# Masked softmax on one core: GpSimd zeroes a slot before, not after, it issues the two whole loads

## The chip, the cores and the metric

The kernel runs on one core of one Trainium2 chip. The metric is the time of one execution on the device in microseconds; lower is better. For a profiled execution the page also gives the span, from the first to the last recorded event.

## The reference

Input `x` has the shape (16, 8, 256, 256), float32; `lengths` holds 16 whole numbers, drawn from 128 to 255. For each batch only the first `lengths[b]` columns take part, the others of the result are zero:

```python
result = np.zeros_like(x)
for b in range(batch):
    length = lengths[b]
    masked = x[b, :, :, :length].copy()
    masked = masked - np.max(masked, axis=-1, keepdims=True)
    exp_masked = np.exp(masked)
    result[b, :, :, :length] = exp_masked / np.sum(exp_masked, axis=-1, keepdims=True)
```

The draw is fixed. The lengths are 188 233 229 243 195 252 165 210 222 180 209 157 159 199 214 248.

## The kernel before, in words

A batch is one tile: 2048 rows, 16 on each of 128 partitions, 256 columns; 2.10 MB. The tile `xt` has 8 slots for such tiles. Batches are worked on by position: positions 0, 1, 2 are batches 1, 2, 3, position 3 is batch 0, and from position 4 on position and batch agree (`batch_of`). Everything is done in place in the slot.

**Loads.** SyncE issues position 0 in two halves (L136), which go through its DMA queue, q1 of the profile. GpSimd issues positions 1 and 2 as whole tiles (L175); its queue is q0. From position 3 on GpSimd loads only as many columns as the batch needs, in steps of 8 or 16 (`pick`, L154): it reads the length, branches to one of several written-out DMAs, and issues it. For such a narrow load the columns from 160 on are first zeroed in the slot (`fill`, L179), once for each of the slots 3 to 7. The zero fill of slot 3 comes after GpSimd has waited for `s_v` to reach 2 (VectorE's two steps L219 and L227, which set up `down` and `len_s`). Position 3 needs slot 3's fill, positions 4 and on need all five fills. In the loop over later positions (L189) a load waits until the load two positions before has landed (`s_sw`), and until the store of the tile that had the slot before has landed (`s_st`).

**Work.** VectorE sets columns past the length to a very low value (`mask`, L236), ScalarE takes the exponential row by row with the row's sum (`rows`, L343, 16 instructions for a tile, in two halves), VectorE takes the reciprocal of the sums (L257) and multiplies (L260, once for each half). VectorE's order is written out: it multiplies position b's first half, masks position b+1, multiplies b's second half; for position 1 the mask comes first. A final check of the sums (L292 to L303) decides on a second, slower path, which is not taken here.

**Stores.** SyncE issues them (L143) in position order, through q1 as well: position 0 in halves, positions 1 to 7 as a half and two quarters, 8 to 12 and 15 in halves, 13 and 14 whole. A store waits for its multiply (`s_out`) and, from position 2 on, for the landing of the store two positions before (L142).

The lines the change touches, in the order of GpSimd's program:

```python
for b in range(1, ahead):
    nc.gpsimd.dma_start(out=xt[:, b], in_=x_f[batch_of(b)]).then_inc(s_ld[b + 1], 16)
nc.gpsimd.wait_ge(s_v, 2)
def fill(b):
    nc.gpsimd.memset(xt[:, b, :, low:], 0.0).then_inc(s_fill, 1)
fill(ahead)
```

with `ahead = 3` and `low = 160`.

Of the kernel before, what the change touches and what calls it, by code (L numbers as in the profile page):

```python
# [21 lines left out]
def kernel(  # L22
# [6 lines left out]
    nc = tc.nc  # L29
# [9 lines left out]
    x_f = x.rearrange("b h q k -> b (h q) k").rearrange("b (p t) k -> b p t k", p=P)  # L39
# [5 lines left out]
    ahead = 3  # L45
    assert ahead == 3 and slots == 8 and batch == 16

    def batch_of(pos):
        return pos + 1 if pos < ahead else 0 if pos == ahead else pos
# [22 lines left out]
    xt = pool.tile([P, slots, nt, seq_k], F32, name="xt")  # L72
# [26 lines left out]
    with tc.tile_critical(no_gpsimd_drain=True):  # L99
# [4 lines left out]
        s_ld = [sem(f"s_ld{k}") for k in range(ahead + 1)]  # L104
# [32 lines left out]
        for b in range(batch):  # L137
            s_b = s_st[b % 2]
            for s in parts(b):
                nc.sync.wait_ge(s_out, 2 * b + (s.stop - 1) // half + 1)  # L140
                if b >= 2 and s.start == 0:
                    nc.sync.wait_ge(s_b, 64 * (b // 2 + 1))  # L142
                nc.sync.dma_start(  # L143
                    out=out_f[batch_of(b), :, s, :], in_=xt[:, b % slots, s, :]
# [26 lines left out]
        nc.gpsimd.memset(ones_c, 1.0).then_inc(s_ones, 1)  # L171
        for par in range(2):
            nc.gpsimd.memset(seed[:, par : par + 1], 0.0).then_inc(s_st[par], 64)  # L173
        for b in range(1, ahead):
            nc.gpsimd.dma_start(out=xt[:, b], in_=x_f[batch_of(b)]).then_inc(s_ld[b + 1], 16)  # L175
        nc.gpsimd.wait_ge(s_v, 2)

        def fill(b):
            nc.gpsimd.memset(xt[:, b, :, low:], 0.0).then_inc(s_fill, 1)  # L179

        fill(ahead)
        nc.gpsimd.wait_ge(s_word, 16)
        nc.gpsimd.wait_ge(s_fill, 1)
        v_len = length(POOL, word[0:1, 0:1])
# [26 lines left out]
        def step(ins):  # L211
# [8 lines left out]
                out=down, in0=iota_i, scalar1=0.5, scalar2=-big, op0=ALU.add, op1=ALU.mult  # L220
# [7 lines left out]
                out=len_s, in0=len_f, scalar1=big, scalar2=None, op0=ALU.mult  # L228
# [65 lines left out]
        for k, (_, _, edge, op) in enumerate(checks):  # L294
            nc.vector.tensor_scalar(  # L295
                out=bad[:, k : k + 1],
# [13 lines left out]
        with nc.vector.Else():  # L310
            with nc.Fori(0, batch, 1, engines=[DVE]) as i:
                nc.vector.wait_ge(g_ld, 16 * i + 16)
                nc.vector.scalar_tensor_tensor(
                    out=g_t,
# [8 lines left out]
                    out=neg_max, in_=g_t, op=ALU.max, axis=AX, negate=True  # L323
# [5 lines left out]
                    out=g_t,  # L329
# [25 lines left out]
        with nc.scalar.If(a_redo >= 1):  # L355
            for par in range(2):
                nc.scalar.wait_ge(s_st[par], 64 * (batch // 2 + 1))
            with nc.Fori(0, batch, 1, engines=[ACT]) as i:
                nc.scalar.dma_start(out=g_t, in_=x_g[:, bass.ds(i, 1)]).then_inc(g_ld, 16)
                nc.scalar.wait_ge(g_v, 3 * i + 2)  # L360
                with nc.Fori(0, nt, 1, engines=[ACT]) as t:
                    e = g_t[:, bass.ds(t, 1), :]
                    nc.scalar.activation(
                        out=e,
                        in_=e,
# [41 lines left out]
```

## Time and profile before

| | |
|---|---|
| median of 3 runs (lowest to highest) | 155.48 us (155.39 to 155.87) |
| the profiled execution | 155.45 us, span 153.8 us |
| VectorE busy | 116.8 us, 76% of the span |
| ScalarE busy | 105.4 us, 69% |
| GpSimd busy | 22.6 us, 15% |
| moved by DMA | 61.57 MB, mean 400 GB/s over the span |
| share of 16 engines: q1 (SyncE), q0 (GpSimd) | 56.4%, 42.0% |
| loads L175, issue to landing | 11.9 and 17.0 us |
| position 0's halves L136, issue to landing | 5.3 and 11.3 us |

Shares are of the whole span. A window of the DMA view gives, for each queue, packets, MB, and the time that its packets took as a share of 16 engines' time in that window. The timeline gives start, duration, engine, line and operation, and in brackets the idle time before it with what ended it.

### The profile page before, as it was taken

How to read it: one execution, taken by the hardware profiler on the slowest of the kernel's cores; microseconds unless marked ns; L12 is line 12 of the kernel's file. 1: busy time of each engine (PE TensorE's matmuls, PEld its weight loads, DVE VectorE, ACT ScalarE, POOL GpSimd, SP SyncE). 2: the span in 40 equal slices, each digit the busy share in tenths (PEclk: the TensorE clock that was granted, in tenths of full speed). 3: DMA queues.
4: the chain of work that ended last, by engine and by line, in shares of the span. 5: the costliest groups of instructions: out<-in, count | busy, mean ns of one | idle time of the engine just before them, and what ended most of it. 6: DMA issues, size and time to landing. Idle time of an engine off the chain costs nothing.

```text
span 153.8 us, 1304 instructions
## 1 busy us (share of the span) xinstructions
PE 0.3 (0%) x2; PEld 0.2 (0%) x2; DVE 116.8 (76%) x91; ACT 105.4 (69%) x514; POOL 22.6 (15%) x30
## 2 busy tenths in 40 slices
PE   0000000000000000000000000000000000000000
PEld 0000000000000000000000000000000000000000
DVE  1206999896969799796969696988969676986900
ACT  3082699959596886959595959779595938869000
POOL 7694100101120200202011020202010000000000
DMA  4999999999999999999999999999999999999993
GB/s 98 435 416 445 367 322 428 415 415 431 426 395 387 425 407 419 411 415 417 395 422 410 415 410 405 409 424 413 423 414 417 419 436 426 424 441 439 426 411 162
DMA packets 10357, 61.57 MB, mean 400 GB/s; under 512 B 866, under 2 KB 978, under 8 KB 6642
## 3 DMA queue, kind: packets, MB, share of 16 engines
q1 hardware_dynamic: 5616, 35.65, 56.4%
q0 software_dynamic: 4736, 25.89, 42.0%
q14 instruction: 3, 0.02, 0.0%
q10 hardware_dynamic: 2, 0.00, 0.0%
HBM read 27.98 MB, written 33.55 MB: 400 GB/s over the span
## 4 chain that ended last, share of the span: by engine, by line
DVE 34%; DMA 29%; ACT 16%; issue 10%; ACTq 4%; SPq 0%; POOLq 0%; PE 0%
DMA xt<-in_x_dram 21%; DVE xt L260 16%; ACT xt L343 16%; DVE xt L236 16%; DMA out_dram<-xt 8%; ACTq L343 4%; DVE inv_sum L257 1%; ACTq L349 1%; DVE ends L292 0%; SPq L136 0%; DVE bad L295 0%; SPq L143 0%; PE count L206 0%; POOLq L159 0%; DVE redo L303 0%
## 5 line engine op out<-in xcount | busy, mean ns | idle before, releaser
L343 ACT ACTIVATE xt<-xt (+1 forms) x256 | 102.4, 401 | 35.2 <-DVE xt L236 35.2
L260 DVE TENSOR_TENSOR xt<-xt,inv_sum 128x2048 f32<-128x2048 f32 x32 | 73.3, 2292 | 1.1
L343 ACT ACTIVATION_READ_ACCUMULATOR xt<-xt (+1 forms) x256 | 47.8, 187 | 0.0
L236 DVE SCALAR_TENSOR_TENSOR xt<-down,len_s,xt 128x2048 f32<-128x2048 f32 (+1 forms) x17 | 37.7, 2220 | 9.7 <-DMA xt<-in_x_dram 9.7
L154 POOL DMA_DIRECT2D xt<-in_x_dram x13 | 13.8, 1062 | 91.3 <-DMA out_dram<-xt 59.7
L257 DVE RECIPROCAL inv_sum<-row_sum 128x8 f32<-128x8 f32 x32 | 6.4, 199 | 16.0 <-ACT xt L343 16.0
L179 POOL MEMSET xt<- 128x1536 f32 x5 | 6.7, 1399 | 0.0
L336 ACT ACT_TABLE_LOAD x1 | 1.3, 1283 | 1.6 <-SPq L99 1.6
L219 DVE TENSOR_SCALAR down<-iota_i 128x256 f32<-128x256 int32 x1 | 0.3, 301 | 1.6 <-POOL iota_i L167 1.6
L175 POOL DMA_DIRECT2D xt<-in_x_dram x2 | 1.2, 604 | 0.0
L292 DVE TENSOR_REDUCE ends<-row_sum 128x1 f32<-128x256 f32 x2 | 0.7, 412 | 0.0
L224 DVE CAST len_b<-word 1x16 bf16<-1x16 int32 x1 | 0.3, 272 | 0.4 <-DMA word<-in_lengths_dram 0.4
L206 PE MATMUL count<-bad,ones_c 128*1 128x3 bf16 x1 | 0.2, 165 | 143.0 <-DVE bad L295 143.0
L227 DVE TENSOR_SCALAR len_s<-len_f 128x16 f32<-128x16 f32 x1 | 0.2, 175 | 0.4 <-PE len_f L204 0.4
L167 POOL IOTA iota_i<- 128x256 int32 x1 | 0.3, 331 | 0.6 <-SPq L99 0.6
L303 DVE TENSOR_REDUCE redo<-count 1x1 f32<-1x3 f32 x1 | 0.1, 148 | 0.3 <-PE count L206 0.3
L295 DVE TENSOR_SCALAR bad<-ends 128x1 bf16<-128x1 f32 x3 | 0.3, 150 | 0.0
L173 POOL MEMSET seed<- 1x1 f32 x2 | 0.2, 225 | 0.0
L206 PEld LDWEIGHTS count<-bad,ones_c 128*1 128x1 bf16 x1 | 0.1, 79 | 143.1 <-DVE bad L295 143.1
L336 ACT ACTIVATE warm<-const-float32-0.0 128x1 f32<-128x1 f32 x1 | 0.2, 203 | 0.0
L170 POOL MEMSET ones<- 1x128 bf16 x1 | 0.2, 194 | 0.0
L204 PE MATMUL len_f<-len_b,ones 1*128 1x16 bf16 x1 | 0.2, 168 | 2.7 <-DVE len_b L224 2.7
(8 smaller groups left out, 0.8 us busy)
## 6 DMA issues: line engine op xcount, KB each, us to landing
out_dram<-xt SPq DMA_DIRECT2D x21, 1024.0 KB
xt<-in_x_dram POOLq DMA_DIRECT2D x4, 2048.0 KB, 15.5
out_dram<-xt SPq DMA_DIRECT2D x14, 512.0 KB
xt<-in_x_dram POOLq DMA_DIRECT2D x3, 1728.0 KB, 16.4
out_dram<-xt SPq DMA_DIRECT2D x2, 2048.0 KB
xt<-in_x_dram POOLq DMA_DIRECT2D x2, 1600.0 KB, 19.2
xt<-in_x_dram POOLq DMA_DIRECT2D x2, 1280.0 KB, 14.2
xt<-in_x_dram SPq DMA_DIRECT2D x2, 1024.0 KB, 8.3
```

What stands on the lines that cost most here:

```text
L154: nc.gpsimd.dma_start(out=xt[:, slot, :, :w], in_=x_n[:, b, :, :w]).then_inc(s_sw[par], 16)
L167: nc.gpsimd.iota(iota_i, pattern=[[1, seq_k]], base=0, channel_multiplier=0).then_inc(s_iota, 1)
L175: nc.gpsimd.dma_start(out=xt[:, b], in_=x_f[batch_of(b)]).then_inc(s_ld[b + 1], 16)
L179: nc.gpsimd.memset(xt[:, b, :, low:], 0.0).then_inc(s_fill, 1)
L206: nc.tensor.matmul(count, lhsT=ones_c, rhs=bad, start=True, stop=True).then_inc(s_count, 1)
L236: return nc.vector.scalar_tensor_tensor(out=t, in0=down[:, None, lo:hi].to_broadcast([P, s.stop - s.start, hi - lo]), scalar=len_s[:, batc ...
L257: step(nc.vector.reciprocal(out=inv_sum[:, b, s], in_=row_sum[:, b, s]))
L260: nc.vector.tensor_tensor(out=t, in0=t, in1=inv_sum[:, b, s, None].to_broadcast([P, half, seq_k]), op=ALU.mult,).then_inc(s_out, 1)
L292: step(nc.vector.tensor_reduce(out=ends[:, k : k + 1], in_=values, op=op, axis=AX))
L336: nc.scalar.activation(out=warm, in_=nc.const_aps.tensor(0.0, (P, 1), F32), func=EXP)
L343: ins = nc.scalar.activation(out=e, in_=e, func=EXP, accum_out=sum_h[:, i, j])
L349: with nc.Fori(1, 2 * batch, 1, engines=[ACT]) as i:
```

## The change

GpSimd first waits for `s_v` and zeroes the columns from 160 on of slot 3, and then issues the two whole loads of positions 1 and 2. After them it goes on as before with the length and the narrow load of position 3, then the other four fills. No instruction is added or removed, on no other engine does the order change.

```diff
             nc.gpsimd.memset(seed[:, par : par + 1], 0.0).then_inc(s_st[par], 64)
+        nc.gpsimd.wait_ge(s_v, 2)
+
+        def fill(b):
+            nc.gpsimd.memset(xt[:, b, :, low:], 0.0).then_inc(s_fill, 1)
+
+
+        fill(ahead)
         for b in range(1, ahead):
             nc.gpsimd.dma_start(out=xt[:, b], in_=x_f[batch_of(b)]).then_inc(s_ld[b + 1], 16)
-        nc.gpsimd.wait_ge(s_v, 2)
-
-        def fill(b):
-            nc.gpsimd.memset(xt[:, b, :, low:], 0.0).then_inc(s_fill, 1)
-
-        fill(ahead)
         nc.gpsimd.wait_ge(s_word, 16)
         nc.gpsimd.wait_ge(s_fill, 1)
```

More of the change, by code (lines that the diff above doesn't have):

```diff
@@ L173 @@
             nc.gpsimd.memset(seed[:, par : par + 1], 0.0).then_inc(s_st[par], 64)
-        for b in range(1, ahead):
-            nc.gpsimd.dma_start(out=xt[:, b], in_=x_f[batch_of(b)]).then_inc(s_ld[b + 1], 16)
         nc.gpsimd.wait_ge(s_v, 2)
@@ L181 @@
         fill(ahead)
+        for b in range(1, ahead):
+            nc.gpsimd.dma_start(out=xt[:, b], in_=x_f[batch_of(b)]).then_inc(s_ld[b + 1], 16)
         nc.gpsimd.wait_ge(s_word, 16)
```

## The prediction

> **What bounds the kernel now.** I read the page first (shares in 40 slices, then the chain), then GpSimd's timeline, the DMA queues in short windows, and the stores as SyncE issues them. The page's two DMA rows:
>
> ```profile
> DMA  4999999999999999999999999999999999999993
> GB/s 98 435 416 445 367 322 428 415 415 431 426 395 387 425 407 419 411 415 417 395 422 410 415 410 405 409 424 413 423 414 417 419 436 426 424 441 439 426 411 162
> ```
>
> The 16 DMA engines are busy from 2 us to the end; VectorE, with 76% of the span, ends at 146.2 while packets move until 152. The kernel is bound by bytes: 61.57 MB. The one weak place is slices 5 and 6 (15.4 to 23.1 us): 367 and 322 GB/s at full busy share. What the change touches is GpSimd's start:
>
> ```profile
> 1.94 1.21 POOL L175 DMA_DIRECT2D xt<-in_x_dram  x2
> 3.17 1.39 POOL L179 MEMSET xt<- 128x1536 f32 x1
> 5.95 1.17 POOL L154 DMA_DIRECT2D xt<-in_x_dram  x1 [1.39 <-issue]
> ...
> 14.66 1.16 POOL L154 DMA_DIRECT2D xt<-in_x_dram  x1 [2.20 <-issue]
> ...
> 38.04 1.16 POOL L154 DMA_DIRECT2D xt<-in_x_dram  x1 [8.17 <-issue]
> ```
>
> The two whole loads (positions 1 and 2, 2.10 MB each) are issued from 1.94, but in the queue windows the GpSimd queue q0 moves nothing before 5.95 and its first packets in 5.95 to 6.05: 4.0 us after the first issue. The load issued at 38.04 met an almost empty q0 and started in 42.85 to 43.2, 4.8 us after its issue, 3.7 after its end. So 3.4 to 3.7 us lie between an issue's end and data while SyncE's queue q1 is busy. From 5.95 to 12.5 q0 moved 2.02 MB and q1 only 0.84, so position 0's second half ended near 12.5 and VectorE started on it at 12.94. Then, first 17.8 to 21.8 us, second 22 to 34:
>
> ```profile
> DMA packets 258, 1.17 MB, mean 293 GB/s; under 512 B 10, under 2 KB 10, under 8 KB 252
> ...
> q0 software_dynamic: 253, 1.13, 95.1%
> q1 hardware_dynamic: 5, 0.04, 2.4%
> ```
>
> ```profile
> DMA packets 855, 5.01 MB, mean 418 GB/s; under 512 B 59, under 2 KB 75, under 8 KB 482
> ...
> q1 hardware_dynamic: 421, 3.08, 61.2%
> q0 software_dynamic: 434, 1.94, 40.1%
> ```
>
> Here is the weak place: position 3's narrow load (rows of 192 columns) runs alone at 293 GB/s, because the first store, issued at 16.69, only shows packets from 20.8 on. Beside stores the sum is 418 GB/s, but a narrow load gets 1.94 MB in 12 us, 0.162 MB/us: one packet of each queue in turn (434 to 421), the store's being the larger. Last, the end, by the loads' last wait on VectorE and by SyncE's stores:
>
> ```profile
> 115.14 2.35 DVE L236 SCALAR_TENSOR_TENSOR xt<-down,len_s,xt 128x2048 f32<-128x2048 f32 x1
> 124.72 2.35 DVE L236 SCALAR_TENSOR_TENSOR xt<-down,len_s,xt 128x2048 f32<-128x2048 f32 x1 [1.12 <-DMA xt<-in_x_dram]
> ```
>
> ```profile
> 137.92 0.36 SPq L143 DMA_DIRECT2D out_dram<-xt  x1
> ...
> 144.79 0.37 SPq L143 DMA_DIRECT2D out_dram<-xt  x1
> ```
>
> Position 14's mask already waits 1.12 us for its load, so any lateness of loads passes whole to all that follows. Position 14's store goes out at 137.92, as its last multiply ends (135.60 + 2.29). The last store goes out at 144.79 with 1.8 MB of older stores still queued (stores issued less q1's moved bytes).
>
> **The change, part by part.** *The wait on s_v moves ahead of the loads.* It ends with the len_s step (2.94 + 0.17 = 3.11); GpSimd is free at about 1.95. Nothing else is queued behind it than the fill, the loads and the narrow loads. *The fill* runs at 3.17 to 4.56 as before. *The two issues* come at 4.56 to 5.77 instead of 1.94 to 3.15: 2.6 us later. *The narrow load of position 3* (length read and branches of 1.39 us, as now) is issued at 7.16 instead of 5.95, the four later fills and position 4's load 1.2 us later too. Both still lie behind 4.19 MB of whole loads in q0, so these cost nothing; without that cover they would cost 1.2 us of load time.
>
> *When q0 starts.* The first issue ends at 4.56 + 0.68 = 5.24; with the 3.4 us of the row, data at 8.6. Until then q1 has all engines. By 6 us q1 had moved 1.25 MB in either kernel; its other 0.85 MB at 0.43 MB/us end at 8.0. So 0 to 0.7 us of idle DMA: none if a new queue's delay is only work queued ahead of it (q1's start from rest took 1.13 to 2.16, only 1.0 us), 0.6 by the rows under load, which I take, being the same queue and issue.
>
> *Position 0.* Its second half lands near 8.4 instead of 12.5. VectorE masks it at 8.4 to 9.7; ScalarE ends the first half at 11.1; the multiply runs 11.4 to 13.7; the first store is issued at 13.75 instead of 16.69. With the delay of before (16.69 to 20.8, 4.1 us) it moves from 17.9.
>
> *What is late next.* Whole loads: 8.6 + 4.19 MB / 0.422 = 18.5 instead of 17.7, 0.8 us late. Position 3's narrow load then has a store beside it nearly from its start. The 1.13 MB that took 4.0 us alone take 1.13 / 0.162 = 7.0: 3.0 us late. Most store packets came yet 0.5 to 1 us after the first, so some of it still runs alone; I take off 0.4. Loads are thus 0.8 + 3.0 - 0.4 = 3.4 us late, at position 3 and, as q1 has no pause from then on and each load is only issued some 1.4 us after the landing of the load two before it, at all later positions. In the middle VectorE has 3 to 5 us between landing and mask and its own start is earlier, so little shows there. At position 14 no slack is left: its mask moves from 124.72 to 128.1.
>
> *The end.* Two bounds. By bytes: the weak place loses (422 - rate) over 17 to 22 us (358, 344, 272, 260 and 311 GB/s in 1 us windows), 565 / 422 = 1.3 us, of which some 0.3 stay; idle DMA costs 0.6. A gain of 0.4, or 1.0 if there is no idle time: last packet 151.1 to 151.7 instead of 152.1. By loads: position 14's store can go at 137.92 + 3.4 = 141.3. Stores have by then got ahead by what the loads lost, so q1 is empty and starts 1.0 us later, as from rest; 4.19 MB (positions 14 and 15) at 0.43 take 9.8, and 0.6 is the tail of uneven engines seen now (151.5 to 152.1): 141.3 + 1.0 + 9.8 + 0.6 = 152.7. The later bound counts: +0.6 us. With late loads of L us the end is 149.3 + L against 152.1: L = 2.8 is break-even.
>
> The profiled execution took 155.45 (1.65 outside its span), its runs' median is 155.48. 155.45 + 0.6 = 156.05, and 0.03 for the median: 156.1.
>
> **The rivals.** *Forecast:* earlier stores cost the narrow load its time alone; L of 2.3 to 4.2, an end of 151.6 to 153.5, 155.0 to 156.9. Chance 0.45.
>
> *Not slower, by bytes:* loads are late by less than 1.8 us, which happens if the first store again needs 5 us or more before its bulk moves (as the rows of 21 to 22.5 us hint), or if the load of position 6 makes up time where q0 now stands empty (40.6 to 42.85). Then the bytes decide and filling the weak place pays: at most 152.1 - 1.0, time 154.5. Against it: the first store goes out 3 us sooner and would have to be delayed by all of that. Chance 0.20.
>
> *Nothing moves:* q0's 4.0 us before first data are not a fixed delay, but the fill at 3.17 to 4.56 holds back GpSimd's descriptors. Then a load issued after the fill, with 0.6 us from issue end to data as q1 had at rest, moves at 5.24 + 0.6 = 5.9, as now at 5.95; position 0's second half shares the engines as before, and the time is 155.5. Against it: the load at 38.04 had no fill behind it and needed 4.8 us. Chance 0.15. The Trainium skill ("DMA: Bandwidth & Descriptors", Specifications) gives a first-byte latency of about 1 us for GpSimd's path; by it, as an estimate, loads would move from 5.6 us on and this rival would hold. The trace's 4.0 and 4.8 us differ from that figure, and I go by them.
>
> *Worse:* the first store starts 1.0 us after its issue as q1 did from rest, at 14.8, while whole loads still run. Their last 3.7 us at 0.425 MB/us, 1.6 MB, then go at two thirds (16 KB packets against 8 KB): 1.8 us more, and nothing of position 3 runs alone: L = 0.8 + 3.0 + 1.8 = 5.6, end 154.9, time 158.3. Against it: the 4.1 us of the first store now. Chance 0.20, for all cases of L over 4.2.
>
> **How the numbers follow.** A measurement of this kernel can tell about 0.3%, 0.47 us, from no change. Faster: the rival by bytes, 0.20, and 0.02 of "nothing moves". Slower: "worse", 0.20, two thirds of the forecast, 0.30, and 0.02 of "nothing moves". Same: 0.15 + 0.11 = 0.26. The range goes from the rival by bytes, 154.5, to the end of "worse", 158.3; the forecast's own is 155.0 to 156.9.
>
> **What would show it right or wrong.** Right: GpSimd's fill ahead of the two issues at 4.6 us; q0's first packet near 8.6; position 0's second mask near 8.4; first store near 13.75; no slice near 322 GB/s; position 3's and 4's masks stalled by loads and position 14's mask near 128; pauses of q1 after 136. Wrong: q0 moving near 6 us (nothing moves); position 14's mask before 126.6 with DMA busy to the end (by bytes); stores beside the whole loads from 15 us (worse).

## The result, and the profile after

The changed kernel takes 156.19 us (median of 7 runs, 155.71 to 156.43) against 155.42 for the kernel before beside it; the ratio is 1.0044, 95% interval 1.0028 to 1.0061. A second series (the run g3 below) gives 1.0030, 1.0018 to 1.0042. So it is slower by 0.5 to 0.7 us. The profiled execution took 156.43 us with a span of 154.7.

First the page's two DMA rows of the changed kernel:

```profile
DMA  4999999999999999999999999999999999999992
GB/s 121 420 430 436 273 420 416 379 410 441 414 401 391 423 406 421 409 415 421 393 421 410 411 415 401 419 411 421 415 419 417 437 430 415 432 447 415 434 417 95
```

The engines are still busy from 2 us to the end. The weak place has moved from slices 5 and 6 to slice 5 alone, 273 GB/s, and there is a new one: slice 8 (27.1 to 30.9 us), 379 GB/s, where before had 415. GpSimd's timeline of the changed kernel:

```profile
3.05 1.39 POOL L177 MEMSET xt<- 128x1536 f32 x1 [1.09 <-DVE len_s L228]
4.37 1.21 POOL L182 DMA_DIRECT2D xt<-in_x_dram  x2
5.83 1.18 POOL L154 DMA_DIRECT2D xt<-in_x_dram  x1 [0.24 <-issue]
...
30.27 0.56 POOL L154 DMA_DIRECT2D xt<-in_x_dram  x1 [14.56 <-issue]
38.31 1.16 POOL L154 DMA_DIRECT2D xt<-in_x_dram  x1 [7.47 <-issue]
44.66 1.15 POOL L154 DMA_DIRECT2D xt<-in_x_dram  x1 [5.19 <-issue]
```

The fill now comes ahead of the two issues. Position 3's narrow load goes out at 5.83, no later than before: the idle time ahead of it, which held the reading of the length, is 0.24 us behind the two issues, where it was 1.39 behind the fill. Compare the three later issues with 29.31, 38.04 and 44.82 of before: 0.96 late, 0.27 late, 0.16 early. The lateness of the loads dies out within three loads. At the end VectorE's masks of positions 13 and 14 stand earlier than before:

```profile
114.10 2.35 DVE L237 SCALAR_TENSOR_TENSOR xt<-down,len_s,xt 128x2048 f32<-128x2048 f32 x1
124.09 2.35 DVE L237 SCALAR_TENSOR_TENSOR xt<-down,len_s,xt 128x2048 f32<-128x2048 f32 x1 [1.52 <-DMA xt<-in_x_dram]
```

The compute chain is not what ends later. The bytes are. Stretches of the DMA view, rate in the last column; before, then after:

```profile
10.00:16.00 6.00, 0.00 (x0) 0.00 (x0) 3.03 (x3) 2.69 (x13) 3.63 (x3) 1.00 1.01 430
16.00:22.00 6.00, 0.00 (x0) 0.00 (x0) 5.96 (x5) 4.63 (x25) 0.00 (x0) 1.00 0.95 323
...
26.00:30.00 4.00, 0.00 (x0) 0.00 (x0) 3.54 (x5) 4.00 (x22) 0.56 (x1) 1.00 1.02 419
```

```profile
10.00:16.00 6.00, 0.00 (x0) 0.00 (x0) 5.49 (x5) 4.18 (x22) 3.52 (x3) 1.00 1.01 415
16.00:22.00 6.00, 0.00 (x0) 0.00 (x0) 3.65 (x3) 5.79 (x29) 0.00 (x0) 1.00 0.96 336
...
26.00:30.00 4.00, 0.00 (x0) 0.00 (x0) 3.97 (x3) 3.81 (x20) 0.00 (x0) 1.00 1.03 380
```

Up to 26 us the two are level: 0 to 10 us gains 0.06 MB (310 against 304 GB/s), 10 to 16 loses 0.09, 16 to 22 gains 0.08. From 26 to 30 us the changed kernel loses 4 us x 39 GB/s = 0.16 MB, and from 34 to 145 us both run at 417. Packets that begin before 145 us carry 58.90 MB before and 58.77 after. And the last engine straggles: after 152.2 us the changed kernel still moves this,

```profile
DMA packets 5, 0.02 MB, mean 13 GB/s; under 512 B 3, under 2 KB 3, under 8 KB 3
...
q1 hardware_dynamic: 5, 0.02, 3.1%
```

where before had ended at 152.1. By the trace's completion packets the 16 engines end at 151.5 (mean) and 152.1 (last) before, at 151.8 and 153.0 after.

### The profile page after: what moved, and what is told of

The parts are those of the page before. It is cut to its first block, busy times and chain, and to the rows that moved or that the text cites. A ratio compares the mean times of both kernels' runs of the same rounds, so it can differ in the third digit from the quotient of the medians.

```text
span 154.7 us, 1304 instructions
## 1 busy us (share of the span) xinstructions
PE 0.3 (0%) x2; PEld 0.2 (0%) x2; DVE 116.9 (76%) x91; ACT 105.5 (68%) x514; POOL 22.6 (15%) x30
## 2 busy tenths in 40 slices
DMA packets 10357, 61.57 MB, mean 398 GB/s; under 512 B 866, under 2 KB 978, under 8 KB 6642
## 4 chain that ended last, share of the span: by engine, by line
DMA 43%; DVE 29%; ACT 10%; issue 7%; ACTq 3%; POOL 1%; POOLq 1%; SPq 0%; PE 0%
DMA xt<-in_x_dram 23%; DMA out_dram<-xt 19%; DVE xt L261 15%; DVE xt L237 12%; ACT xt L344 10%; ACTq L344 3%; DVE inv_sum L258 1%; POOL xt L177 1%; DMA word<-in_lengths_dram 1%; DVE ends L293 0%; ACTq L350 0%; POOLq L126 0%; SPq L143 0%; DVE bad L296 0%; DVE len_s L228 0%
```

## The experiments

Unless it says otherwise, a ratio is to the kernel before on the same chip, with its 95% interval; MB are those of packets begun before 145 us. They say how far a kernel has got with its 61.57 MB; at the 425 GB/s of 100 to 145 us, 0.43 MB are 1 us.

**e1: the changed kernel, position 1's first multiply ahead of position 2's mask.**

```diff
-            first = b != 1
+            first = True
```

> The changed kernel, with position 1's first multiply ahead of position 2's mask, as for all other positions. Empty-queue theory (the changed kernel loses its time where SyncE's queue q1 stands empty, 27.5 to 29.0 us, because position 1's first store only goes out at 25.5): that store goes out near 21.7, q1 has no pause near 27.5, and 0.3 to 0.8 us come back: 155.4 to 155.9. Late-loads theory (the prediction's: loads beside stores come late up to position 14): q0 loses the time it had alone, position 3's load lands later still, 156.2 to 157. In both ScalarE waits some 1.6 us for position 2's mask.

Measured: 155.9 us, 1.0022 (1.0011 to 1.0034). Position 1's first store goes out at 22.07 instead of 25.53. In the window 27.5 to 29 us the changed kernel and this one have:

```profile
DMA packets 129, 0.51 MB, mean 340 GB/s; under 512 B 14, under 2 KB 26, under 8 KB 129
...
q0 software_dynamic: 129, 0.51, 102.2%
```

```profile
DMA packets 101, 0.62 MB, mean 410 GB/s; under 512 B 3, under 2 KB 7, under 8 KB 52
...
q1 hardware_dynamic: 49, 0.40, 64.2%
q0 software_dynamic: 52, 0.21, 35.8%
```

In the changed kernel q1 is empty there: it has run dry at 27.5, and the store issued at 25.53 shows its first packet at 29.0. In e1 it is busy, 26 to 30 us run at 419 GB/s as before, and 58.94 MB are moved by 145 us. The loads are late, as the late-loads theory says, with position 14's mask at 126.22; the kernel is still not slower than the changed one. So the pause costs bytes, and late loads of this size cost none. In time the gain over the changed kernel (1.0044 and 1.0030) is not clear of noise.

**e2: the same edit on the kernel before.**

> The kernel before, with the same edit of VectorE's order. Its q1 had no pause after 20.8 us, so by the empty-queue theory nothing is gained: 155.2 to 155.7. By the late-loads theory position 1's store is some 2 us earlier beside the same loads: 155.5 to 156. If the order of VectorE alone is worth something, both this and the changed kernel with it move by the same amount.

Measured: 155.75 us, 1.0013 (1.0001 to 1.0025), 58.92 MB; 26 to 30 us at 421 GB/s. Nothing gained, as the empty-queue theory says: there was no pause to close. With this edit on both sides the change costs 1.0022 / 1.0013 = 1.0009, which is within noise.

**e3 and g1: an early small write.** A tile of zeros is written to rows that the last store overwrites, in e3 through ScalarE's queue, in g1 through q1. Of e3 only the write is shown here; the tile, its zeroing and the last store's wait for this write are left out.

```diff
+        nc.scalar.wait_ge(s_zed, 1)
+        nc.scalar.dma_start(out=out_f[batch - 1, :, nt - 1, 0:64], in_=zed).then_inc(s_tiny, 16)
```

> The kernel before, plus a 32 KB write of zeros (256 bytes for each partition, into rows of the output that the last store overwrites) which ScalarE issues at about 1.6 us, ahead of any other write. First-write theory (the stretch at 270 to 300 GB/s from about 2 to 5 us after the first store's issue belongs to the first writes of the program): the slow stretch at 17.8 to 21.8 shrinks and up to 1.0 us comes back, 154.4 to 155.0. Narrow-load theory (the prediction's: a narrow load alone runs at 293 GB/s): unchanged, 155.2 to 155.7. If a queue that starts anew is what costs, unchanged too.

> The kernel before, plus a 128 KB write of zeros (1 KB for each partition, into rows that the last store overwrites) which SyncE issues through q1 itself, right behind position 0's two loads, long before the first real store. If the slow stretch that follows the first store's issue belongs to the first write of this queue, it moves to where this write falls (near 12 us) or goes away, and 17.8 to 21.8 us run at 340 GB/s or more: 154.4 to 155.2 if it goes, 155.4 to 156.0 if it only moves. If it belongs to the large store itself, nothing changes: 155.5 to 156.0 (the added bytes cost 0.3).

Measured: e3 155.71 us, 1.0011 (0.9996 to 1.0026); g1 155.98 us, 1.0012 (0.9998 to 1.0025). The slow stretch stays where it was; e3 from 18 to 20 us:

```profile
DMA packets 127, 0.56 MB, mean 281 GB/s; under 512 B 5, under 2 KB 5, under 8 KB 127
...
q0 software_dynamic: 127, 0.56, 97.1%
```

g1 has 252 GB/s there. The stretch does not belong to the first write of the program as such, nor to the first of this queue.

**e4: the changed kernel, position 0's first half stored only when both halves are ready.**

```diff
-                nc.sync.wait_ge(s_out, 2 * b + (s.stop - 1) // half + 1)
+                nc.sync.wait_ge(s_out, 2 * b + (s.stop - 1) // half + 1 if b else 2)
```

> The changed kernel, with position 0's first half stored only when both halves are ready (18.4 us instead of 13.5). If the slow stretch belongs to the first store, it moves from 16 to 19.5 us to about 21 to 24 and the whole loads of positions 1 and 2 run at 420 GB/s to their end near 17.7. If it belongs to the loads, it stays or begins where position 3's narrow load begins. Time: by the late-loads theory the loads gain and it falls to 155.0 to 155.7; by the empty-queue theory q1 starts later but then has no pause, 155.4 to 156.2.

Measured: 155.76 us, 1.0014 (1.0005 to 1.0023), 59.10 MB, the most of all kernels. In the changed kernel the whole loads are slowed from 15.5 to 19.5 us, as its first store (13.48) waits to move:

```profile
DMA packets 98, 1.14 MB, mean 285 GB/s; under 512 B 8, under 2 KB 8, under 8 KB 14
...
q0 software_dynamic: 66, 0.88, 77.9%
q1 hardware_dynamic: 31, 0.25, 15.0%
```

With the first store at 18.43 the same whole loads run at 414 GB/s from 15.5 to 17.5, and 15 of 16 engines end them by 18.1 (19.9 in the changed kernel). So in this kernel what slowed the whole loads came with the early first store. Position 3's narrow load, now alone, has 341 GB/s from 18 to 20 and 325 from 20 to 22: alone it is slow too, but less so than the 293 on which the prediction was built.

**h1 and h2: the same edit on the kernel before, and on f1.**

> The kernel before with position 0's first half stored only when both halves are ready (near 21.4 instead of 16.7 us). With the changed kernel that edit put 0.27 MB more into the first 145 us, since q1 no longer ran empty a second time. Before had no second pause, so by the bytes nothing is to be gained: the slow stretch moves on to 21 to 25 us, position 3's narrow load runs alone longer, and the time is 155.4 to 156.2. If a late first store is good in itself, 154.9 to 155.4.

> The kernel with the wait alone moved (loads issued at 3.3 us), with position 0's first half stored only when both halves are ready (near 19.5). Position 0 and 1 start early and q1 starts once. If the bytes moved by 145 us set the time, it gains as the changed kernel did from this edit, 0.1 MB or more over before: 155.0 to 155.5. If the uneven end or the later stores eat that, 155.5 to 155.9.

Measured: h1 155.98 us, 1.0022 (1.0012 to 1.0031), 58.92 MB. h2 155.74 us, 1.0002 (0.9992 to 1.0013), 59.00 MB. (e4 had 0.33 MB more than the changed kernel, 59.10 against 58.77, not the 0.27 of the expectation.) h2 was the version to which the bytes pointed; it is no faster than before, nor is any other. In both the last engine ends 1.2 us after the mean of the 16; that the uneven end takes up what the bytes gain is argued, not shown. h1 is a miss for the bytes: it moves as much as before and is slower by 0.3 us. Late loads do not explain that, since position 14's mask starts 1.2 us earlier than before (123.56), without a wait. With this edit on both sides (e4, h1) the change costs 1.0014 / 1.0022 = 0.9992, again within noise.

h1 also shows the narrow load alone on both sides of the first store's issue, which is now at 21.42:

```profile
20.00:22.00 2.00, 0.00 (x0) 0.00 (x0) 2.00 (x2) 2.00 (x12) 0.00 (x0) 1.00 1.05 332
22.00:24.00 2.00, 0.00 (x0) 0.00 (x0) 1.97 (x3) 2.00 (x12) 0.00 (x0) 1.00 1.01 330
```

The kernel before has 285 GB/s from 20 to 22. In h1 the rate does not fall after the store's issue, nor does it in e4 (issue at 18.43) and h2 (330 GB/s from 19.6 to 23). So a deep stretch does not come with the first store wherever that falls.

**f1: the wait alone is moved.**

```diff
+        nc.gpsimd.wait_ge(s_v, 2)
         for b in range(1, ahead):
             nc.gpsimd.dma_start(out=xt[:, b], in_=x_f[batch_of(b)]).then_inc(s_ld[b + 1], 16)
-        nc.gpsimd.wait_ge(s_v, 2)
```

> One part of the change alone: GpSimd waits for s_v ahead of the two whole loads, but the zero fill of slot 3 stays behind them, so the loads are issued at about 3.1 instead of 1.9 (before) or 4.4 us (changed). If the start of q0 follows the issue by a fixed 3.2 to 4 us, its first packet comes at 6.3 to 7.1; position 0's second half then still shares the engines, the first store goes out near 15 to 16, and the time lies between the two kernels, 155.5 to 156.0. If the change costs by an early first store alone, it is nearer to before, 155.4 to 155.7.

Measured: 155.66 us, 1.0005 (0.9995 to 1.0015). Loads issued at 3.30, q0's first packet at 7.2, first store at 14.79, no pause of q1 later, 58.94 MB. Here the lateness does reach position 14, whose mask waits longer and starts 1.6 us later than before:

```profile
126.34 2.35 DVE L236 SCALAR_TENSOR_TENSOR xt<-down,len_s,xt 128x2048 f32<-128x2048 f32 x1 [3.27 <-DMA xt<-in_x_dram]
```

It costs nothing that can be measured, as the break-even of 2.8 us in the prediction's own sum would have it. A wait alone, 1.4 us of later issue, is free; with the fill ahead as well (another 1.1 us) q1 pauses.

**f4: three fills ahead of the loads.**

```diff
         fill(ahead)
+        fill(ahead + 1)
+        fill(ahead + 2)
```

The later loop fills the other two slots only.

> The changed kernel with three fills ahead of the two loads instead of one: loads issued at about 7.0 instead of 4.4 us. Fixed delay (3.2 us from issue to data): q0 starts at 10.2, the engines stand idle from 8.0 to 8.9 until then, 0.6 to 0.9 MB are lost, and since the kernel is bound by bytes the time is 157.6 to 158.4. If the delay only lasts while q1 has work queued, q0 starts about 1 us after its issue, at 8.0 to 8.5, and the time stays at 156.0 to 156.8.

Measured: 157.22 us, 1.0100 (1.0085 to 1.0115), between the two expectations. From 8.0 to 10.2 us:

```profile
8.00:10.20 2.20, 0.00 (x0) 0.00 (x0) 1.28 (x1) 2.20 (x13) 2.20 (x3) 1.00 0.84 212
```

The changed kernel has 406 there. f4 has moved 58.26 MB by 145 us: 0.64 MB less than before, and 0.64 / 0.43 = 1.5 us, against 1.6 measured. This is the bytes' price in its clearest form: some 0.46 MB of it are lost here (before has 421 GB/s), and 0.16 from 26 to 30 us (379 against 419), where q1 stands empty again, from 28.3 to 30.3. q0's first packet comes at 8.4, 1.4 us after the issue (7.00) and just as q1 has run dry at 8.3; from 10.2 to 14 us it has 414 GB/s. The Trainium skill ("DMA: Bandwidth & Descriptors", Specifications) gives about 1 us for GpSimd's first byte. The trace comes near that only here, with little work left ahead; behind q1 it was 4.0, 3.9 and 3.2 us (before, f1, changed).

**f2: SyncE issues the two whole loads behind position 0's, in q1.**

```diff
+        for b in range(1, ahead):
+            nc.sync.dma_start(out=xt[:, b], in_=x_f[batch_of(b)]).then_inc(s_ld[b + 1], 16)
```

GpSimd's two issues are left out.

> The kernel before, but SyncE issues the whole loads of positions 1 and 2 right behind position 0's, so they go through q1 in that order; GpSimd loads from position 3 on, as before. Queue-restart theory (a q1 that has run empty needs 3.5 to 4 us until its next packet, and meanwhile all engines move at 270 to 340 GB/s): q1 is busy from 2 us to the end, there is no slow stretch, position 0 is complete near 8.4 us, 1.0 to 1.2 us are gained: 154.2 to 154.6. First-store theory (any first store slows the engines for some 3 us, wherever it falls): the stretch comes when the first store's packets start, near 20 us, and the time stays 155.2 to 155.8.

Measured: 155.81 us, 1.0006 (0.9995 to 1.0017). q1 is busy from 2 us on, and yet from 19 to 22 us:

```profile
DMA packets 126, 0.89 MB, mean 297 GB/s; under 512 B 15, under 2 KB 15, under 8 KB 77
...
q1 hardware_dynamic: 64, 0.61, 62.3%
q0 software_dynamic: 62, 0.29, 26.4%
```

A queue that starts anew is thus not needed for a slow stretch. What makes it stays open: in f4 the first store goes out at 13.52, as in the changed kernel (13.48), and yet from 15.5 to 19.5 us it has 391 GB/s, where the changed kernel has 285.

**g3 and i1: the changed kernel and the kernel before, once more.**

> The changed kernel itself once more, timed beside the same runs of before, for its bytes moved by 145 us and its uneven end. By the bytes alone (0.13 MB behind before at 145 us) it is 0.3 us slower than before; by the first measurement 0.7. If the uneven end of the DMA engines is chance, this profile's last packet comes nearer to the others and the ratio is about 1.002 to 1.003; if it belongs to the changed order, the end is uneven again by some 1.2 us over the mean and the ratio is 1.004 or more.

> The kernel before itself once more, for a second profile of its end. In the first its 16 DMA engines ended at 151.5 us on the mean and the last one 0.6 us after that; in the changed kernel's two profiles the last one came 1.0 and 1.2 after the mean of 151.8. If the even end belongs to the order of before, it is 0.5 to 0.8 again. If it is chance, it is 0.9 or more, and of the difference between the two kernels only the 0.3 us of the mean end (0.13 MB) has a cause. The ratio shows how far two equal kernels come apart: 0.999 to 1.001.

Measured: g3 156.18 us, 1.0030 (1.0018 to 1.0042), 58.76 MB; i1 155.52 us, 0.9994 (0.9984 to 1.0004), 58.99 MB. From 26 to 30 us, first g3, then i1:

```profile
26.00:30.00 4.00, 0.00 (x0) 0.00 (x0) 3.97 (x3) 3.87 (x20) 0.00 (x0) 1.00 1.03 382
```

```profile
26.00:30.00 4.00, 0.00 (x0) 0.00 (x0) 3.58 (x3) 4.00 (x22) 0.46 (x1) 1.00 1.02 419
```

The loss in this stretch is there in both profiles of the changed kernel and in neither of before. On the mean of two profiles each, the changed kernel has moved 0.18 MB less by 145 us, 0.4 us, and its engines' mean end is 0.4 us later (151.83 against 151.43). The last engine comes 0.6 and 0.9 us after the mean before, 1.2 and 0.95 in the changed kernel: on the mean 0.3 us more, with as much between two profiles of the same kernel.

## Why the prediction was right or wrong

It said 156.1 us, slower, and 156.19 was measured. The value and the direction held; the path by which it got there did not.

*GpSimd's order and the issues.* Right: fill at 3.05, issues from 4.37 (predicted 3.17 and 4.56). Wrong in a detail: position 3's load is not 1.2 us later (5.83 against 5.95).

*When q0 starts.* Predicted 8.6 with 0.6 us of idle DMA; it was 7.5, and no time was lost, 421 GB/s from 7.5 to 8.9. The lower bound given there, that the delay is work queued ahead, was the better one: the delay shrinks from 4.0 to 1.4 us as q1's remaining work shrinks (before, f1, changed, f4). The rival "nothing moves" is refuted: here the fill is over at 4.44, and q0 starts at 7.5, not near 5.9.

*Position 0 and the first store.* First store at 13.48 (predicted 13.75): right, though the second mask came 0.9 us later than forecast, at 9.32. The worse rival's early start of that store did not come: its packets begin at 16.9 and in bulk at 17.8.

*What is late next.* The whole loads ended 1.1 to 1.7 us later (0.8 predicted). Position 3's load was late on most engines: by the trace's completion packets 15 of 16 had it at 28.1 instead of 25.4. But a load counts when its last engine is done, and before had one engine 2.1 us behind the others. As a whole the load landed at 28.9 (5.83 + 23.1) instead of 27.95 (5.95 + 22.0): 1.0 late, not 3.4, and position 5's load, which waits for it, went out 0.96 late. The reason was half wrong too. The slow stretch is only in part the narrow load's own (about 330 GB/s alone in h1): a deep one struck the whole loads once the first store came earlier (285 GB/s), so it was moved and not filled. The step "565 / 422 = 1.3 us, of which some 0.3 stay" is thereby wrong: from 16 to 22 us only 0.08 MB came back.

*"As q1 has no pause from then on and each load is only issued ... after the landing of the load two before it, at all later positions."* This is the step that failed. q1 does pause, from 27.5 to 29.0: position 2's mask (20.71, after 2.31 us of waiting for its load) stands ahead of position 1's multiply, so that position 1's store goes out only at 25.53, 0.56 earlier than before, while position 0's stores went out 3 us earlier:

```profile
20.71 2.35 DVE L237 SCALAR_TENSOR_TENSOR xt<-down,len_s,xt 128x2048 f32<-128x2048 f32 x1 [2.31 <-DMA xt<-in_x_dram]
22.98 0.20 DVE L258 RECIPROCAL inv_sum<-row_sum 128x8 f32<-128x8 f32 x1
23.21 2.29 DVE L261 TENSOR_TENSOR xt<-xt,inv_sum 128x2048 f32<-128x2048 f32 x1
```

In the pause the narrow load catches up, and the rest is absorbed at position 6, where q0 had stood empty before as well (the rival by bytes had named that place). L at position 14 was -0.6 us, not 3.4. Even without the pause the lateness does not last: in e1 position 3 lands 3.0 us later than before (5.82 + 25.1), and 1.5 us of it are left at position 14. The signs that the prediction named say the same: the masks of positions 3 and 4 (30.30 and 38.68) do not wait, q1 has no pause after 136 us, and a mask of position 14 before 126.6 with DMA busy to the end was its sign for the rival by bytes.

*The end.* The bound "by loads", 152.7, was not the one that counted; the bound by bytes was, and it stood on the wrong side: not 0.4 us gained, but 0.4 lost. With 0.3 of a more uneven end this gives 0.7, the size forecast. That the two sums agree is luck. The break-even of 2.8 us is not contradicted: e1 and f1 have their loads 1.5 and 1.6 us late at position 14 and move as many bytes as before (58.94 MB). No run came nearer to it.

What is shown: the changed kernel loses 0.16 MB in the pause of q1. Two different edits take the pause away (e1, e4) and bring these bytes back, and beside the same edit on the kernel before (e2, h1) the change costs nothing clear of noise, 1.0009 and 0.9992, each known to about 0.002. What stays open: why kernels with equal bytes still differ by 0.1 to 0.2% (e2, h1 against before), and with it the uneven end of the engines. No run changed that end alone.

## What to carry to other kernels

In a kernel bound by bytes, ask of every shift which queue will run dry, and when the next transfer on it is issued: here a store 3 us earlier was worth nothing, since the store after it came no earlier and the queue between them stood empty. A slow stretch seen beside one kind of transfer need not belong to it alone; move the other candidate (here the first store), look at the rate on both sides of its new place, and allow that both have a part. An edit that closes a gap can cost something itself, so try it on the kernel before as well. And a lateness is worth only what is left over after the places where its queue stands empty anyway.

## What the runs showed of the hardware that was not expected

In the kernel before and in the changed one the issue of the first store (16.69 and 13.48) is followed, 1 to 2 us later, by 3 to 4 us in which the DMA engines are nearly always busy (0.95 of the time and more) and move about 290 GB/s instead of 420: narrow loads in the one (292 from 18 to 21 us), whole tiles in the other (285 from 15.5 to 19.5). An earlier small write does not prevent it (e3, g1). It does not come with every first store: with both halves stored together (e4, h1, h2) the narrow load keeps 321 to 337 GB/s behind the issue, and f4 has 391 from 15.5 to 19.5. The cause is open.

The delay from a GpSimd issue to its first packet was 4.7 (f2, 5.92 to 10.65), 4.0, 3.9, 3.2 and 1.4 us, the shorter the less SyncE's queue still had to move. And the last of the 16 DMA engines ends 0.6 to 1.5 us after their mean; in a kernel that is 155 us long this is as much as the change was worth.
